# The opening of a two-layer diffusion backbone: x loaded first, modulation blocks into free buffers, the norm in two halves among three projections

## The chip, the cores and the metric

The kernel runs on one core of a Trainium2 chip. The metric is the device time of one execution in microseconds, as the median of some runs; lower is better. The engines are TensorE (PE, with its weight loads as PEld), VectorE (DVE), ScalarE (ACT), GpSimd (POOL) and SyncE (SP, which here issues most of the DMAs). SBUF holds the tiles, PSUM takes the products of PE.

## The reference, cut to what matters

Two layers over 512 latent tokens and, in the first layer, 256 context tokens, 1024 channels wide. The opening of a layer is a modulated RMSNorm and one wide input projection:

```python
sc = jax.nn.silu(c)
scc = jax.nn.silu(c_ctx)
sh1, sc1, g1, sh2, sc2, g2 = [m[:, None, :] for m in jnp.split(sc @ ada_w[l] + ada_b[l], 6, axis=-1)]
csh1, csc1, cg1, csh2, csc2, cg2 = jnp.split(scc @ ada_w[l] + ada_b[l], 6, axis=-1)
hl = rms_norm(xl, norm1_g[l]) * (1.0 + sc1) + sh1
hc = rms_norm(xc, norm1_g[l]) * (1.0 + csc1) + csh1
pl = jnp.split(hl @ w_in, IN_OFFSETS, axis=-1)   # and hc @ w_in
```

Three token mixers (window attention, a bidirectional mLSTM, a Hyena long convolution whose filters are computed from a small sine network) use the projections; their outputs are gated, merged and projected, and a convolutional feed-forward follows. The second layer has no context at its end.

## The kernel before, in words

Activations lie with channels on the partitions: x is 8 tiles (k = 0 to 7) of 128 channels by 768 tokens, columns 0 to 511 latent, 512 to 767 context. Each projection (`proj`, `gemm_part`) takes one tile of 128 output channels: a weight of 128 x 1024 is loaded (`raw`, L392), split into a rounded part wh on ACT (L342) and a rest wl on DVE (L343), and multiplied with the like parts hh and hlo of the normed x. That makes three matmuls for each k (`kstep`, L406), 24 for the 512 latent columns and 24 shorter ones for the 256 context columns.

The modulation vectors are products of silu(c) with the blocks of ada_w. A block has 512 outputs; blocks 0 and 1 are the shift, 2 and 3 the scale of the first norm, for k = 0 to 3 and 4 to 7. `ada` (L478) computes one block: four loads of 512 KB through the four buffers "wr", eight matmuls in four column groups of the array, a copy (L482), four transposes (L486) and a sum on DVE (L489); `ada_end` makes A = (1 + scale) * g (L500). The other blocks of the layer come later, row by row on DVE (`ada_rows`, L514), and read silu(c) from `silb`, which holds it along the free axis on all partitions.

The opening of the first layer (`main`) loads x on GpSimd's queue (L1677), runs blocks 0, 2, 1, 3, with the sums of squares behind block 0, the norm of k = 0 to 3 behind block 2 and of k = 4 to 7 behind block 3, and then `proj_first`: three projections, two of them k by k together and the third behind them, then the context columns of all three. Squares of the latent columns run on ACT, of the context columns on GpSimd (`SQP`).

Beside this, lanes of other work are spent in program order. A lane is a generator that yields its cost; `tick` counts the PE time of what was just issued and lets each lane run on by that time multiplied by its rate. The lane `filters` (rate 1.587 in the first layer) builds the Hyena filters: two sine stages (L594 to L606), then for each of four units of two lengths the taps (`filter_taps`: L693 and L694 on PE, times a decay on DVE L681, absolute values on ACT L685, their sum on GpSimd L689, a matmul with ones L700, a reciprocal L703) and the transform (`filter_dft`, L749), whose sums go to DRAM as gd (L766). The lane `ml_gates` (L1258 to L1350) makes the mLSTM's gates. In the opening, where no projection runs, the table START says what each yield of `ada` counts as. From program order a scheduler makes the order of each engine's queue; each engine runs its queue in order.

The first layer's gate phase ends with the pool "mixa0" (tags T and H); the attention projections write their first tile, k (L773), in the pool that takes its place, once every tile of the old pool is done with. The PSUM pool "psg" has three banks for projections.

Of the kernel before, what the change touches and what calls it, by code (L numbers as in the profile page):

```python
# [11 lines left out]
F32 = mybir.dt.float32  # L12
F32R = mybir.dt.float32r
BF16 = mybir.dt.bfloat16
AF = mybir.ActivationFunctionType
# [226 lines left out]
class Prog:  # L242
# [5 lines left out]
    START = (0.8, 0.5, 0.2, 0.8)  # L248
# [106 lines left out]
    clock = 0.0  # L355

# [38 lines left out]
    def weight(self, src, n=1024):  # L395
        raw = self.raw(src, n)
# [27 lines left out]
    def proj_first(self, l, ms, parts):  # L424

        ws = [self.weight(self.a["wA"][l, m]) for m in ms]
# [4 lines left out]
        for i, (lo, hi, _) in enumerate(parts):  # L431
# [3 lines left out]
            for group in ((0, 1), (2,)) if i == 0 else ((0,), (1,), (2,)):  # L435
                for k in range(KD):
                    for j in group:
                        self.kstep(pss[j], ws[j], slice(k * P, k * P + P), self.hlh[k], self.hll[k], lo, hi, k == 0, k == KD - 1)
                    self.tick(3 * len(group) * max(0.109, (hi - lo) * 0.422e-3))
            for o, ps in zip(outs, pss):  # L440
                o.append((lo, hi, ps))
# [28 lines left out]
    def ada(self, l, blocks):  # L470

        nc = self.nc
        for b in blocks:
            ps = self.M("adap")
            for q in range(2):
                aw = [self.raw(self.a["adaw"][b, 2 * q + j]) for j in range(2)]
                for g in range(4):
                    nc.tensor.matmul(ps[32 * g:32 * g + 32, :], self.sil[:, 4 * q + g, :],  # L478
                                     aw[g // 2][:, (g % 2) * 512:(g % 2) * 512 + 512], start=(q == 0), stop=(q == 1))
                yield 6.0  # L480
            ev = self.H("adae")
            nc.scalar.copy(ev, ps)  # L482
            yield 1.5
            p2 = self.M("adaq")
            for c in range(4):
                nc.tensor.transpose(p2[:, c * P:(c + 1) * P], ev[:, c * P:(c + 1) * P], self.ident)  # L486
            yield 1.0
            m = self.mod[l][:, b * 4:b * 4 + 4, :]
            nc.vector.tensor_reduce(m, p2.rearrange("p (c g r) -> p c r g", g=4, r=32)[:, :, 0:2, :], axis=AX.X, op=ALU.add)  # L489
            self.ada_end(l, b, 2)  # L490
# [1165 lines left out]
    def main(self, out):  # L1656
# [3 lines left out]
        for l in range(DEPTH):  # L1660
# [7 lines left out]
            with tc.tile_pool(name=f"mixa{l}", bufs=1) as self.mp, self.psum(5) as self.pm:  # L1668
                self.nT, self.nH = self.SIZES[f"A{l}"]
                if l == 0:  # L1670
# [5 lines left out]
                    for k in range(KD):  # L1676
                        nc.gpsimd.dma_start(x[k], xd[:, k, :])  # L1677
# [137 lines left out]
```

## Time and profile before

| | us |
|---|---|
| three runs: median (lowest to highest) | 2728.38 (2725.72 to 2732.3) |
| profiled execution, its own time | 2726.24 |
| its span, first to last instruction | 2724.2 |
| PE busy | 2570.0 (94%) |
| DVE busy | 1890.5 (69%) |
| ACT busy | 1039.2 (38%) |
| GpSimd busy | 298.9 (11%) |

A share is an average over the whole span. The page also cuts the span into 40 slices of 68 us; PE's digits are 5 in the first slice and 8 in the second, and 9 in most of the others. A window of the trace gives the same for any stretch, with the clock that PE was granted in it as a share of 2.4 GHz. In a timeline row the bracket at the end says how long the engine had been idle before, and what released it.

### The profile page before, as it was taken

Reading aid. Unit: us, or ns where it says so; the run is one execution under the profiler, and the core shown is the slowest. Engines: PE = TensorE matmul, PEld = TensorE weight load, DVE = VectorE, ACT = ScalarE, POOL = GpSimd, SP = SyncE. Lnnn points to the kernel's source line nnn. Section 1 sums busy time; section 2 is a strip of 40 time slices with the busy share of each in tenths; the row PEclk is TensorE's granted clock in tenths of the full one; section 3 lists DMA queues with packets and bytes.
Section 4 is the critical chain, followed back from the end, with each engine's and each line's share of the span. In section 5 each row is a group of like instructions: output and inputs, shape, how many; then the busy total and the mean of one; then the engine's idle time right before and its main releaser. Section 6 shows DMA issues by size and latency. Waiting matters only on the chain. (4 is left out here: it accounts for less than half of the span.)

```text
span 2724.2 us, 37645 instructions
## 1 busy us (share of the span) xinstructions
PE 2570.0 (94%) x14338; PEld 2171.1 (80%) x14338; DVE 1890.5 (69%) x3317; ACT 1039.2 (38%) x1874; POOL 298.9 (11%) x305
## 2 busy tenths in 40 slices
PE   5898999999999998999999998999998989999998
PEld 2677788888787787888888887877887878888887
DVE  6796676677567856978877657766376577666656
ACT  4333344455322224433333235444354233533333
POOL 3352120000000301101101001310000002000000
PEclk8899999999999998999999999999999999999999
DMA  7344452232547531343434225543335565233332
GB/s 266 111 144 138 157 138 63 63 107 96 192 149 244 187 111 39 115 127 93 125 107 124 78 62 189 184 130 101 93 121 181 178 213 185 78 93 100 94 100 62
DMA packets 153795, 349.97 MB, mean 128 GB/s; under 512 B 15681, under 2 KB 53038, under 8 KB 153488
## 3 DMA queue, kind: packets, MB, share of 16 engines
q1 hardware_dynamic: 132976, 319.03, 36.2%
q0 software_dynamic: 20640, 28.54, 4.2%
q8 instruction: 113, 1.85, 0.3%
q14 instruction: 66, 0.54, 0.1%
HBM read 288.59 MB, written 52.17 MB: 125 GB/s over the span
## 5 line engine op out<-in xcount | busy, mean ns | idle before, releaser
L406 PE MATMUL pg<-hh,wh 128*128 128x512 f32 (+1 forms) x2536 | 916.6, 362 | 21.1 <-ACT hh L342 11.0
L406 PE MATMUL pg<-hlo,wh 128*128 128x512 f32 (+1 forms) x2536 | 903.0, 356 | 2.9 <-DVE hlo L343 2.8
L406 PE MATMUL pg<-hh,wl 128*128 128x512 f32 (+1 forms) x2536 | 901.0, 356 | 0.3 <-DVE wl L343 0.3
L406 PEld LDWEIGHTS pg<-hh,wh 128*128 128x128 f32 x2536 | 484.4, 191 | 87.2 <-ACT hh L342 12.5
L342 ACT CAST wh<-wr 128x1024 fp32r<-128x1024 f32 x294 | 308.8, 1050 | 615.0 <-PE pg L406 580.4
L406 PEld LDWEIGHTS pg<-hlo,wh 128*128 128x128 f32 x2536 | 485.8, 192 | 65.0 <-DVE hlo L343 5.2
L406 PEld LDWEIGHTS pg<-hh,wl 128*128 128x128 f32 x2536 | 484.4, 191 | 64.8 <-issue 1.6
L343 DVE TENSOR_TENSOR wl<-wr,wh 128x1024 fp32r<-128x1024 f32 x294 | 366.1, 1246 | 190.5 <-ACT wh L342 185.6
L1570 DVE SCALAR_TENSOR_TENSOR x<-pg,mod,x 128x512 f32<-128x512 f32 (+1 forms) x242 | 148.2, 628 | 102.2 <-PE pg L406 96.1
L406 PE MATMUL pg<-fh,wh 128*128 128x512 f32 (+1 forms) x544 | 193.4, 356 | 11.7 <-DVE x L1570 10.3
L406 PE MATMUL pg<-fl,wh 128*128 128x512 f32 (+1 forms) x544 | 191.7, 353 | 0.0
L406 PE MATMUL pg<-fh,wl 128*128 128x512 f32 (+1 forms) x544 | 190.5, 351 | 0.9 <-DVE wl L343 0.9
L781 ACT ACTIVATE u<-pg,sv 128x512 f32<-128x512 f32 (+1 forms) x165 | 116.1, 706 | 102.3 <-PE pg L406 102.0
L782 DVE SCALAR_TENSOR_TENSOR u<-pg,sv,u 128x511 f32<-128x511 f32 (+1 forms) x165 | 108.1, 657 | 64.4 <-ACT u L781 64.3
L406 PEld LDWEIGHTS pg<-fh,wh 128*128 128x128 f32 x544 | 103.7, 191 | 30.7 <-DVE x L1570 13.7
L514 DVE SCALAR_TENSOR_TENSOR wr<-wr,silb 128x1024 f32<-128x1024 f32 x80 | 98.3, 1229 | 36.8 <-DMA wr<-in_adat 36.4
L406 PEld LDWEIGHTS pg<-fh,wl 128*128 128x128 f32 x544 | 103.7, 191 | 15.1 <-DVE wl L343 1.4
L406 PEld LDWEIGHTS pg<-fl,wh 128*128 128x128 f32 x544 | 104.0, 191 | 13.9 <-issue 0.5
L406 PE MATMUL pg<-bh,wh 128*128 128x512 f32 (+1 forms) x320 | 111.1, 381 | 3.7 <-DVE y L1556 2.0
L783 DVE SCALAR_TENSOR_TENSOR u<-pg,sv,u 128x511 f32<-128x511 f32 (+1 forms) x165 | 108.5, 660 | 2.1
L1111 ACT ACTIVATE p<-s,sm 128x512 f32<-128x512 f32 (+2 forms) x80 | 55.2, 689 | 128.9 <-DVE sm L1108 100.2
L406 PE MATMUL pg<-bh,wl 128*128 128x512 f32 (+1 forms) x256 | 94.4, 369 | 0.0
(315 smaller groups left out, 4085.1 us busy)
## 6 DMA issues: line engine op xcount, KB each, us to landing
wr<-in_wA SPq DMA_DIRECT2D x222, 512.0 KB, 3.6
wr<-in_adat SPq DMA_DIRECT2D x80, 512.0 KB, 3.6
wr<-in_wD SPq DMA_DIRECT2D x48, 512.0 KB, 3.7
wr<-in_wB SPq DMA_DIRECT2D x24, 512.0 KB, 4.7
gates<-gt SPq DMA_DIRECT2D x28, 384.0 KB, 2.3
gc<-in_g POOLq DMA_DIRECT2D x40, 256.0 KB, 3.5
g<-gd SPq DMA_DIRECT2D x40, 256.0 KB, 4.4
g<-gates SPq DMA_DIRECT2D x24, 384.0 KB, 5.9
```

The costliest lines, as they stand in the source:

```text
L342: nc.scalar.copy(h, src)
L343: (nc.gpsimd if pool else nc.vector).tensor_tensor(l, src, h.bitcast(F32), op=ALU.subtract)
L406: self.nc.tensor.matmul(ps[:, :hi - lo], a[:, ks], b[:, lo:hi], start=(first and i == 0), stop=(last and i == 2))
L514: nc.vector.scalar_tensor_tensor(prod, aw, 1.0, self.silb[:, v, :], op0=ALU.mult, op1=ALU.mult, accum_out=self.mod[l][:, b * 4 + c, v:v + 1])
L781: nc.scalar.activation(dst[:, lo:hi], ps[:, :n], AF.Identity, bias=b, scale=w(1))
L782: V(dst[:, lo + 1:hi], ps[:, 0:n - 1], w(0), dst[:, lo + 1:hi], op0=mul, op1=add)
L783: V(dst[:, lo:hi - 1], ps[:, 1:n], w(2), dst[:, lo:hi - 1], op0=mul, op1=add)
L1111: nc.scalar.activation(t[:, :w], src, AF.Exp, bias=sm[:, 2 + j:3 + j], scale=0.125, accum_out=sm[:, 4 + j:5 + j])
L1570: self.nc.vector.scalar_tensor_tensor(x[m][:, lo:hi], ps[:, :hi - lo], self.mod[l][:, p * 8 + m, j:j + 1], x[m][:, lo:hi], op0=ALU.mult, o ...
```

## The change

The opening of the first layer becomes a function `start`, and `ada` is cut in three (`ada_load`, `ada_products`, `ada_take`). x is loaded on SP's queue, ahead of all blocks. All four blocks are loaded at once into buffers that are free then: block 0 into "wr", block 2 into "wh" and "wl", block 1 into eight "HL" tiles, block 3 into eight "T" tiles; the first three weights are issued ahead of block 3. The products of block 0 come before the sums of squares, the norm of the latent columns of k = 0 to 3 follows blocks 0 and 2. `proj_first` takes the three projections together, k outermost, and calls hooks behind k = 0 (the products of block 3), k = 1 (its modulation, the latent norm of k = 4 to 7 and the norm of all context columns) and k = 7 (constants and the lane of the other blocks). `silb` is no longer computed: the finished silu(c) is written to DRAM and read back to all partitions. START has one entry, used once.

```diff
-    START = (0.8, 0.5, 0.2, 0.8)
+    START = (0.8,)
...
-    def weight(self, src, n=1024):
-        raw = self.raw(src, n)
+    def weight(self, src, n=1024, raw=None):
+        raw = self.raw(src, n) if raw is None else raw
...
-    def proj_first(self, l, ms, parts):
-
-        ws = [self.weight(self.a["wA"][l, m]) for m in ms]
+    def proj_first(self, l, ms, parts, hooks=None):
+
+
+        raws = self.early or [None] * 3
+        self.early = None
+        ws = [self.weight(self.a["wA"][l, m], raw=r) for m, r in zip(ms, raws)]
...
-            for group in ((0, 1), (2,)) if i == 0 else ((0,), (1,), (2,)):
+            for group in ((0,), (1,), (2,)) if i else ((0, 1, 2),) if hooks else ((0, 1), (2,)):
                 for k in range(KD):
                     for j in group:
                         self.kstep(pss[j], ws[j], slice(k * P, k * P + P), self.hlh[k], self.hll[k], lo, hi, k == 0, k == KD - 1)
                     self.tick(3 * len(group) * max(0.109, (hi - lo) * 0.422e-3))
+                    if i == 0 and hooks and k in hooks:
+                        hooks[k]()
...
+    def ada_load(self, b, tiles):
+
+        parts, k = [], 0
+        for t in tiles:
+            n = t.shape[1] // 512
+            o = (k % 2) * 512
+            self.nc.sync.dma_start(t, self.a["adaw"][b, k // 2, :, o:o + n * 512])
+            parts += [t[:, i * 512:i * 512 + 512] for i in range(n)]
+            k += n
+        return parts
+
+    def ada_products(self, aw):
+
+        ps = self.M("adap")
+        for k in range(KD):
+            g = k % 4
+            self.nc.tensor.matmul(ps[32 * g:32 * g + 32, :], self.sil[:, k, :], aw[k], start=(k < 4), stop=(k >= 4))
+        return ps
+
+    def ada_take(self, l, b, ps):
+        nc = self.nc
+        ev = self.H("adae")
+        nc.scalar.copy(ev, ps)
+        p2 = self.M("adaq")
+        for c in range(4):
+            nc.tensor.transpose(p2[:, c * P:(c + 1) * P], ev[:, c * P:(c + 1) * P], self.ident)
+        m = self.mod[l][:, b * 4:b * 4 + 4, :]
+        nc.vector.tensor_reduce(m, p2.rearrange("p (c g r) -> p c r g", g=4, r=32)[:, :, 0:2, :], axis=AX.X, op=ALU.add)
...
     def silu_rows(self):
-        nc = self.nc
-        nc.gpsimd.dma_start(self.silb.rearrange("p v k -> p (v k)"), self.a["cb"].rearrange("v k -> (v k)").partition_broadcast(P))
+
+        nc = self.nc
+        d = self.dp.tile([2, D], F32, name="sild")
         for v in range(2):
-            s = self.silb[:, v, :]
-            t = self.wp.tile([P, 1024], F32, tag="wr", name=self.uid("wr"), bufs=self.WB[0])
-            nc.scalar.activation(t, s, AF.Tanh, scale=0.5)
-            nc.vector.scalar_tensor_tensor(s, t, 1.0, s, op0=ALU.add, op1=ALU.mult)
-            nc.vector.tensor_scalar(s, s, 0.5, None, op0=ALU.mult)
+            nc.gpsimd.dma_start(d[v].rearrange("(k p) -> p k", p=P), self.sil[:, :, v])
+        nc.gpsimd.dma_start(self.silb.rearrange("p v k -> p (v k)"), d.rearrange("v k -> (v k)").partition_broadcast(P))
...
+    def start(self, xd):
+
+        nc = self.nc
+        lat, cx = self.parts(0)
+        x = [self.T("x") for _ in range(KD)]
+        for k in range(KD):
+            nc.sync.dma_start(x[k], xd[:, k, :])
+        wt = lambda tag, n: [self.wp.tile([P, 1024], F32, tag=tag, name=self.uid(tag), bufs=self.WB[tag != "wr"]) for _ in range(n)]
+        aw = {}
+        aw[0] = self.ada_load(0, wt("wr", 4))
+        aw[2] = self.ada_load(2, wt("wh", 3) + wt("wl", 1))
+        aw[1] = self.ada_load(1, [self.hp.tile([P, NT], F32, tag="HL", name=self.uid("aw"), bufs=16)[:, :512] for _ in range(KD)])
+        self.early = [self.raw(self.a["wA"][0, m]) for m in (M_MO, M_MO + 1, M_MO + 2)]
+        aw[3] = self.ada_load(3, [self.T("aw")[:, :512] for _ in range(KD)])
+        self.tick(self.START[0])
+        p0 = self.ada_products(aw[0])
+        self.silu_rows()
+        sums = [self.square_sums(x, lo, hi, self.SQP[j]) for lo, hi, j in self.parts(0)]
+        rs = self.rstd_of(sums)
+        p2 = self.ada_products(aw[2])
+        self.ada_take(0, 0, p0)
+        low, high = range(0, 4), range(4, 8)
+        ts = {k: self.norm_scale(x, lat, rs[0], k) for k in low}
+        self.ada_take(0, 2, p2)
+        self.hlh, self.hll = [None] * KD, [None] * KD
+        for k in low:
+            self.hlh[k], self.hll[k] = self.HL("hh"), self.HL("hlo")
+        self.norm_part(0, 1, x, lat, rs[0], low, ts)
+        p1 = self.ada_products(aw[1])
+        self.ada_take(0, 1, p1)
+        state = {}
+
+        def products():
+            state["p"] = self.ada_products(aw[3])
+
+        def rest():
+            th = {k: self.norm_scale(x, lat, rs[0], k) for k in high}
+            self.ada_take(0, 3, state["p"])
+            for k in high:
+                self.hlh[k], self.hll[k] = self.HL("hh"), self.HL("hlo")
+            self.norm_part(0, 1, x, lat, rs[0], high, th)
+            self.norm_part(0, 1, x, cx, rs[1])
+
+        def then():
+            self.load_consts()
+            self.spawn(1 / 15, self.ada_rows(0, range(4, 12)), stays=True)
+
+        return {0: products, 1: rest, 7: then}
...
-                    x = [self.T("x") for _ in range(KD)]
-                    for k in range(KD):
-                        nc.gpsimd.dma_start(x[k], xd[:, k, :])
-                    self.norm_alloc()
-                    for i, b in enumerate((0, 2, 1, 3)):
-                        for _ in self.ada(0, (b,)):
-                            self.tick(self.START[i])
-                        if i == 0:
-                            rs = self.rstd_of([self.square_sums(x, lo, hi, self.SQP[j]) for lo, hi, j in self.parts(0)])
-                        if i % 2:
-                            for r, part in zip(rs, self.parts(0)):
-                                self.norm_part(0, 1, x, part, r, range(2 * i - 2, 2 * i + 2))
-                    self.load_consts()
-                    self.silu_rows()
-                    self.spawn(1 / 15, self.ada_rows(0, range(4, 12)), stays=True)
+                    hooks = self.start(xd)
```

GpSimd (POOL) at its opening, before; sv, fg, maskb are constants, sq the squares of the context columns:

```order
L301 DMA sv_86<-in_sv 128x305 [waits DMASW0_49]
L302 DMA fg<-in_fg 128x8 [waits DMASW1_49]
L303 DMA maskb<-in_masks 128x256 [waits DMASW2_49]
L523 DMA silb<-in_cb 128x2048 [waits DMASW3_49]
L540 TENSOR_TENSOR sq_219<-x_122 128x256
L540 TENSOR_TENSOR sq_221<-x_123 128x256
```

and now:

```order
L540 DMA sild<-sil 128x8x1 [waits DVE_49] x2
L302 DMA fg<-in_fg 128x8
L303 DMA maskb<-in_masks 128x256
L541 DMA silb<-sild 128x2048 [waits DMASW2_49,DMASW1_49]
L552 TENSOR_TENSOR sq_237<-x_122 128x256 [waits DMAHW5_49]
L552 TENSOR_TENSOR sq_239<-x_123 128x256 [waits DMAHW6_49]
```

The load of x is gone from this queue, and the squares stand behind the read of silb, which waits for the two writes sild.

PE around the first three projections, before; adap is a block's product, adaq its transposes, pm with w3h and w3l the filter's taps, pg the projections:

```order
L478 MATMUL adap_359<-wr_384,sil 32x512
L693 MATMUL pm_390<-w3h_378,hd_348 128x512 [waits DVE_49,PE_49,Activation_49]
L694 MATMUL pm_390<-w3l_379,hd_348 128x512 [waits DVE_49]
L693 MATMUL pm_399<-w3h_378,hd_348 128x512 [waits PE_49]
L694 MATMUL pm_399<-w3l_379,hd_348 128x512
L486 MATMUL adaq_402<-ident,adae_393 128x128 [waits Activation_49]
L486 MATMUL adaq_402<-ident,adae_393 128x128 x3
L693 MATMUL pm_412<-w3h_378,hd_348 128x512 [waits PE_49]
L694 MATMUL pm_412<-w3l_379,hd_348 128x512
L406 MATMUL pg_488<-hh_138,wh_472 128x512 [waits Activation_49]
L406 MATMUL pg_488<-hlo_146,wh_472 128x512
```

and now:

```order
L407 MATMUL pg_354<-hh_304,wh_342 128x512 [waits Activation_49]
L407 MATMUL pg_354<-hlo_305,wh_342 128x512 [waits DVE_49]
L407 MATMUL pg_355<-hh_304,wh_346 128x512 [waits Activation_49]
L407 MATMUL pg_355<-hlo_305,wh_346 128x512
L407 MATMUL pg_354<-hh_304,wl_343 128x512 [waits DVE_49]
L407 MATMUL pg_354<-hh_306,wh_342 128x512
L407 MATMUL pg_354<-hlo_307,wh_342 128x512
L492 MATMUL adap_371<-aw_176,sil 32x512 [waits DMAHW0_49,PE_49]
L407 MATMUL pg_355<-hh_304,wl_347 128x512 [waits DVE_49]
L407 MATMUL pg_356<-hh_304,wh_350 128x512 [waits Activation_49]
L407 MATMUL pg_356<-hlo_305,wh_350 128x512
L407 MATMUL pg_356<-hh_304,wl_351 128x512 [waits DVE_49]
```

The taps have moved behind the latent projections, and the products of block 3 (adap_371) stand among the matmuls of k = 0 and 1.

PE at the end of the filter lane (pp with sdh and sdl is its last transform; pg_2731 and pg_2761 are k's projection in before, pg_2830 the context part of v's projection now), before:

```order
L749 MATMUL pp_2548<-sdl_2523,gc_2077 128x256 [waits DVE_49]
L749 MATMUL pp_2548<-sdh_2522,gc_2079 128x256
L749 MATMUL pp_2548<-sdh_2522,gc_2095 128x256
L749 MATMUL pp_2548<-sdl_2523,gc_2095 128x256
L749 MATMUL pp_2548<-sdh_2522,gc_2097 128x256
L406 MATMUL pg_2731<-hh_144,wh_2727 128x512
L406 MATMUL pg_2731<-hlo_152,wh_2727 128x512
L406 MATMUL pg_2731<-hh_144,wl_2728 128x512
L406 MATMUL pg_2731<-hh_145,wh_2727 128x512
L406 MATMUL pg_2731<-hlo_153,wh_2727 128x512
L406 MATMUL pg_2731<-hh_145,wl_2728 128x512
```

and now:

```order
L765 MATMUL pp_2607<-sdh_2577,gc_2125 128x256
L765 MATMUL pp_2625<-sdh_2596,gc_2146 128x256 [waits Activation_49]
L765 MATMUL pp_2625<-sdl_2597,gc_2146 128x256 [waits DVE_49]
L765 MATMUL pp_2625<-sdh_2596,gc_2148 128x256
L765 MATMUL pp_2625<-sdh_2596,gc_2164 128x256
L765 MATMUL pp_2625<-sdl_2597,gc_2164 128x256
L765 MATMUL pp_2625<-sdh_2596,gc_2166 128x256
L407 MATMUL pg_2830<-hh_304,wh_2801 128x256 [waits Activation_49]
L407 MATMUL pg_2830<-hlo_305,wh_2801 128x256
L407 MATMUL pg_2830<-hh_304,wl_2802 128x256
```

The last transform has moved from the middle of k's projection to behind the latent part of v's, and the next projection waits for ACT.

## Rows read from the trace of the kernel before

**Rows 1.** Windows: busy us of PE, PEld, DVE, ACT, POOL, granted clock, DMA share, GB/s.

```profile
0.00:59.20 59.20, 32.75 (x98) 9.67 (x99) 33.76 (x70) 27.96 (x44) 17.26 (x30) 0.87 0.75 273
59.20:82.60 23.40, 20.59 (x78) 15.73 (x76) 19.39 (x26) 10.13 (x19) 10.91 (x8) 0.90 0.25 83
82.60:98.30 15.70, 6.87 (x29) 6.26 (x29) 10.02 (x17) 4.72 (x9) 6.48 (x7) 0.67 0.35 85
...
120.00:200.00 80.00, 74.85 (x441) 63.85 (x440) 76.66 (x112) 30.37 (x46) 37.78 (x26) 1.00 0.41 138
200.00:240.00 40.00, 29.13 (x145) 23.26 (x145) 28.35 (x62) 18.17 (x31) 7.36 (x3) 0.87 0.35 117
240.00:320.00 80.00, 76.09 (x428) 63.75 (x426) 58.35 (x77) 25.62 (x43) 15.62 (x15) 1.00 0.47 148
320.00:345.10 25.10, 25.02 (x150) 22.38 (x151) 11.05 (x17) 5.82 (x11) 2.44 (x3) 1.00 0.52 173
```

**Rows 2.** Windows of the opening, and DMA queues (packets, MB, share of 16 engines).

```profile
10.00:20.00 10.00, 5.84 (x14) 0.67 (x16) 2.41 (x7) 0.00 (x0) 5.80 (x10) 1.00 1.04 396
...
q1 hardware_dynamic: 132976, 319.03, 36.2%
q0 software_dynamic: 20640, 28.54, 4.2%
```

**Rows 3.** Timeline of the opening: start us, us, engine, line, operation, [idle before, releaser].

```profile
3.09 19.12 SPq L392 DMA_DIRECT2D wr<-in_adaw  x8
...
34.41 1.92 PE L478 MATMUL adap<-wr,sil 128*32 128x512 f32 x16
...
36.43 0.58 ACT L482 COPY adae<-adap 128x512 f32<-128x512 f32 x1 [0.61 <-PE adap L478]
...
56.60 1.04 ACT L342 CAST wh<-wr 128x1024 fp32r<-128x1024 f32 x1 [2.03 <-DMA wr<-in_wA]
...
57.91 1.22 DVE L343 TENSOR_TENSOR wl<-wr,wh 128x1024 fp32r<-128x1024 f32 x1
...
59.62 0.63 PE L406 MATMUL pg<-hh,wh 128*128 128x512 f32 x1
```

**Rows 4.** Timeline, two projection matmuls one behind the other.

```profile
62.28 0.39 PE L406 MATMUL pg<-hh,wl 128*128 128x512 f32 x1
...
62.51 0.39 PE L406 MATMUL pg<-hh,wh 128*128 128x512 f32 x1
```

**Rows 5.** Timeline, the filter lane: a sine's first step, first tap, sums, first DFT.

```profile
33.05 0.81 DVE L594 TENSOR_SCALAR sa<-pm,sv 128x512 f32<-128x512 f32 x1
...
54.14 0.80 PE L693 MATMUL pm<-w3h,hd 128*128 128x512 f32 x1 [1.32 <-ACT w3h L342]
...
75.56 1.29 POOL L689 TENSOR_TENSOR ab<-ab,ab 128x512 f32<-128x512 f32 x1 [0.26 <-ACT ab L685]
...
91.62 0.55 PE L749 MATMUL pp<-sdh,gc 128*128 128x256 f32 x1 [8.84 <-DMA gc<-in_g]
```

**Rows 6.** Timeline, GpSimd's squares of the context columns.

```profile
12.66 3.46 POOL L540 TENSOR_TENSOR sq<-x 128x256 f32<-128x256 f32 x6
```

**Rows 7.** Timeline, mLSTM state transposes, end of the filter lane, transposes of v.

```profile
227.68 1.84 PE L1338 MATMUL pm<-mlst,ident 64*128 64x6 f32 x16
...
309.87 1.13 PE L700 MATMUL pm<-ab,ones 128*128 128x512 f32 x2 [0.40 <-POOL ab L689]
...
324.04 0.28 PE L749 MATMUL pp<-sdh,gc 128*128 128x256 f32 x1
...
328.31 0.86 ACT L773 COPY k<-pg 128x512 f32<-128x512 f32 x2 [5.19 <-DMA gd<-ghi]
...
345.09 0.82 PE L863 MATMUL pm<-ident,v 128*128 128x128 f32 x6
```

More of the change, by code (lines that the diff above doesn't have):

```diff
@@ L355 @@
     clock = 0.0
+    early = None
     def tick(self, us):
@@ L468, in ada_prepare @@
             nc.vector.tensor_scalar(self.sil[:, :, j], t[:, j * 8:j * 8 + 8], 0.5, None, op0=ALU.mult)
-    def ada(self, l, blocks):
-        nc = self.nc
[L473 to L490, printed above, removed]
+    def ada_load(self, b, tiles):
[14 more added lines that the diff above has]
+    def ada_take(self, l, b, ps):
+        nc = self.nc
+        ev = self.H("adae")
[5 more added lines that the diff above has]
+        nc.vector.tensor_reduce(m, p2.rearrange("p (c g r) -> p c r g", g=4, r=32)[:, :, 0:2, :], axis=AX.X, op=ALU.add)
+        self.ada_end(l, b, 2)
     def ada_end(self, l, b, n):
@@ L568, in norm_alloc, with norm_scale, norm_part @@
         self.hlh, self.hll = [self.HL("hh") for _ in range(KD)], [self.HL("hlo") for _ in range(KD)]
-    def norm_part(self, l, i, x, part, r=None, ks=range(KD)):
+    def norm_scale(self, x, part, r, k):
+        lo, hi, _ = part
+        t = self.H("nx")[:, :hi - lo]
+        (self.nc.gpsimd if k % 2 else self.nc.vector).tensor_tensor(t, x[k][:, lo:hi], r[:, :hi - lo], op=ALU.mult)
+        return t
+    def norm_part(self, l, i, x, part, r=None, ks=range(KD), ts=None):
         nc = self.nc
@@ L577, in norm_part @@
         for k in ks:
-            t = self.H("nx")
-            t = t[:, :n]
-            (nc.gpsimd if k % 2 else nc.vector).tensor_tensor(t, x[k][:, lo:hi], r[:, :n], op=ALU.mult)
+            t = ts[k] if ts else self.norm_scale(x, part, r, k)
             a, b = A[:, k, j:j + 1], sh[:, k, j:j + 1]
@@ L1674, in main @@
                     self.tick(0.1)
[L1675 to L1689 removed]
+                    hooks = self.start(xd)
                 else:
+                    hooks = None
                     xc = [Two(None, self.H("xc")) for _ in range(KD)]
@@ L1695, in main @@
                     self.spawn(1 / 11, self.ada_rows(l, range(4, 12)), stays=True)
-                first = self.proj_first(l, (M_MO, M_MO + 1, M_MO + 2), self.parts(l))
+                first = self.proj_first(l, (M_MO, M_MO + 1, M_MO + 2), self.parts(l), hooks)
                 self.gate_proj(l, gates, range(0, 3), first)
```

## The prediction

> **What bounds the kernel now.** I read the table of engines first: TensorE (PE) is busy 94% of the span, so outside the opening an edit gains only what it takes off PE's own queue. The row of 40 slices then shows the one place where PE is not full, its first slice. The windows over that place [rows 1] say how much: of the first 59.2 us PE idles 26.5 us, it idles 8.8 of the 15.7 us before 98.3 us, and between 200 and 240 us it idles 10.9 of 40. The clock column matters as well: 0.87, 0.90, 0.67 and again 0.87 in these windows, against 1.00 elsewhere, so part of the busy time runs at the lower of the two levels (1.2 GHz). The same rows show VectorE (DVE) busy 76.66 of 80 us between 120 and 200 us: in the first layer's gate phase DVE is the second bound, and whoever brings PE there earlier meets it.
>
> The timeline of the opening tells why PE starts late. The first projection matmul stands at 59.62 us [rows 3]. Before it come four modulation blocks, two at a time through four buffers, whose loads (2.1 MB a block) wait for the products that free the buffers; then the normed x, then the three weights.
>
> **1. The first projection matmul, from 59.6 to 37 us.** After the change SyncE issues x, then block 0, block 2, block 1, the three weights and block 3, with no buffer to wait for except that the weights follow block 0's products. SP's first big load was issued at 3.09 us [rows 3]; x now stands there. Transfers ran at 396 GB/s once both queues were full [rows 2]. x is 3.1 MB and three blocks are 6.3 MB: 9.4 / 0.396 = 24 us, so block 1 is read at 27 us. I add 2 us to landing and 3 us for the small writes discussed below: 32 us. Block 2 comes 7 us earlier, which leaves the first half of the norm its 8 us. Behind block 1 stand its last pair of products (1 us), the copy (0.58), the table load and sine of the filter (about 2) and the first weight's cast (1.04) [rows 3]: 36.6, say 37 us. The weights themselves (1.6 MB, 4 us of transfer) land just ahead of their casts. What is late next is the second weight half on DVE (1.22 us each, three of them [rows 3]).
>
> **2. From there to the mLSTM transposes, which stand at 227.68 us [rows 7].** PE's order has the same count of matmul columns before that point in both programs (299,600 and 300,200, counted from the rows of the order), so I compare what lies between. Before: 168.1 us for 275,000 columns, which at 0.226 us for 512 [rows 4] is 121.5 us; 46.6 us are lost, of them 28 us idle by the windows [rows 1], the rest low clock, the few matmuls on plain fp32 and short ones. After: from 37 us there remain 284,000 columns, 125 us, since block 3 and the filter's second stage now come after the first projection matmul. Losses after, one by one:
> - Block 3's eight products stand singly among the matmuls. Eight together took 1.92 us [rows 3]; singly they cost between that and eight times 0.96. I take 5, of which 1.8 is in the columns: +3.2.
> - Low clock after the pause before them, as the first matmul of before had it (0.63 us long, 0.39 later [rows 3, 4]): +2.5. Bounds 0 and 5.
> - The second half of the norm. Block 3's modulation now waits on DVE behind the sine chain of the filter's second stage: eight operations of 0.4 to 0.8 us [rows 5], 5 us after that stage's product, which itself stands behind the woven matmuls. I put PE's wait at +4 (bounds 0 and 8).
> - The filter's first taps. Four pairs of tap matmuls now stand together behind the latent projections; the sum over four tiles on GpSimd (three adds, 1.3 to 1.5 us) must end before the ones-matmul, which PE has in front of the context half: +6.5 and low clock again, +2. In before the like wait is the 8.84 us before 91.6 us [rows 5]; it goes.
> - Behind this, DVE's stretch as before: 5 us idle to 200 us, 9 us after it and about 4 us of low clock [rows 1], with the remaining small matmuls 7 us: +25.
>
> That is 125 + 43 = 168, so the transposes come at 205: 22.7 us earlier. DVE allows it: it starts its dense stretch about as much earlier, and 9 us of its work (two units of filter output, a modulation product) have moved behind this point.
>
> **3. From there to the transposes of v at 345.09 us [rows 7], where both orders have counted 520,320 columns.** Here part is given back. The spending of filter steps is paced by counted PE time. Before, 16 ticks of the four blocks (four each of 0.8, 0.5, 0.2 and 0.8 us in the table START, 9.2 us) drove the filter lane before the first projection; after it is one tick of 0.8 us. So the lane ends 8.4 us of PE work later: its last matmul stands at column 473,700 in before and 495,400 after. Behind the lane stands the end of the buffer pool: the copy of k, the first tile of the next pool, waits for the last filter output to be written. Before, that copy waited 5.19 us for this write and came at 328.31 us, 4 us after the last filter matmul at 324 us [rows 7], and it cost PE nothing: 55 matmuls (9.6 us) stood between, and PE was busy 25.02 of 25.10 us [rows 1]. After, nothing stands between: the next matmul in PE's order needs the bank that this copy frees. The wait is 4.6 us, from that last matmul's end at 324.3 to the end of the first copy, near 328.9. In front of it the last filter matmuls wait for their chain: from the ones-matmul at 309.87 to the last at 324.2 us it took 14 us with other DVE work between its steps; I take 10 to 14 again. PE now has 5.6 us of other work in that time (18 projection matmuls and the transform itself), so it waits 4 to 8. I take 10 us for both; the low clock behind it costs as much as the low clock of 228 to 240 us in before, up to 1 us less. So 22.7 - 10 + 1.3 = 14 us remain at 345 us. Behind it both orders are alike, and so is the rest of the time.
>
> **The sum.** The profiled execution took 2726.24 us (span 2724.2, 2.0 around it), close to the median of 2728.38. 2726.2 - 14 = 2712 us. Own range of this case: 2704 to 2721.
>
> **The one cost without a row.** The vector silu(c) is now written to DRAM and read back as rows: 2 x 1,024 elements of 4 bytes on GpSimd's queue. GpSimd then waits for them before it issues the read, and the eight squares of the context columns (3.46 us for six [rows 6]) stand behind that wait; PE's order has the sums over these squares ahead of block 2's products. So the wait has no price as long as the writes land by about 20 us. The average packet of that queue took 4.2% x 16 x 2724 / 20,640 = 89 ns [rows 2], bytes included. At nothing per element they land near 8 us. At 89 ns, and each taking turns with a packet of the bulk loads (119 ns by the like division of the other queue's 36.2% over 132,976), 128 on each engine take 27 us from 6 us on: 33 us. I take about 20: no wait, 3 us of engine time.
>
> The Trainium skill says in DMA: Bandwidth & Descriptors, Specifications, that transfers under 512 bytes are done as read-modify-write, which speaks against this write; by that rule alone the price lies toward the upper end, as in the second rival. The same page, Queues, rings and completion order, says that an engine drains a whole packet of several descriptors from one ring before it turns to the next; by that the small writes would be through after a few turns, as in the forecast. No row here shows a write of 4 bytes.
>
> **Rivals.**
> - The head start is kept. If the filter lane's end is not late enough to be waited for (DVE runs the last units faster than I allow), the 10 us are not lost: about 2701 us. For it: DVE idles 27% of 240 to 320 us [rows 1]. Against: the copy of k waits for a write whatever DVE does. Chance 0.2.
> - The small writes hold GpSimd to 33 us. Squares to 38, sums, block 2's products, its modulation at 44, the first projection at 52: 15 us of the head start go. 2727 us, no change. For it the 89 ns; against it that a few turns may do. Chance 0.18.
> - Slower: the filter lane runs by its own chain, not by PE. Its second stage's product stands behind block 3 now, so its first taps start at 67 us (37, 72 matmuls of 0.226, the first three losses above, and 4 for the gates' tanh and the cast of the filter weight) instead of 54.14 [rows 5], 13 us later. If its units then take as long as before, it ends at 337 us; the copy of k at 342, the transposes of v after 11 us of matmuls more: 353 instead of 345.1, so 2735 us. It decides once the lane loses more than 5 us against before. Against it: its units were stretched by a full DVE and PE, and get DVE earlier now. Chance 0.12.
>
> **How the numbers follow.** The forecast has 0.5. About 0.2% (5.5 us) is what a measurement of this kernel can tell from no change, so faster means under 2723 and slower over 2734. Faster: nearly all of the forecast's 0.5, the first rival's 0.2 and a little of the second, 0.70. Same: the second rival's most and edges of the others, 0.18. Slower: the third, 0.12. The range takes in the first rival's value with some room and the second's: 2697 to 2731.
>
> **What would show it.** Right: first projection matmul near 37 us; squares on GpSimd ended before 25 us; a PE wait of 4 to 6 us at the second half's first matmul and of 5 before the ones-matmul; the transposes of the mLSTM state near 205 us; a wait of about 5 us for the copy of k just behind the last filter matmul; the transposes of v near 331 us, and nothing new behind them. Wrong: squares that start after 25 us (second rival), no wait at the copy of k (first), first taps late and k copied after 340 us (third).

## The result, and the profile after

The changed kernel is slower: 2753.18 us median (2748.2 to 2758.79, four runs) against 2728.81, a ratio of 1.0090 (95% interval 1.0066 to 1.0113), some 24 us. The forecast was 2712 us, with a chance of 0.12 for slower. The profiled execution took 2752.36 us, its span is 2750.3, 26.1 more than before. Some sixteen of these are there at the transposes of v (360.7 us against 345.09 [rows 7]), the other ten come behind them, where nothing was expected.

Windows of the changed kernel, columns as in [rows 1]; the first two are, within 0.4 us, the stretches up to the first projection matmul and from there to the first tap of the filter:

```profile
0.00:48.40 48.40, 17.85 (x70) 5.04 (x70) 25.04 (x46) 17.44 (x27) 18.94 (x28) 0.97 0.96 300
48.40:80.70 32.30, 27.32 (x94) 15.21 (x94) 18.27 (x39) 16.21 (x30) 0.00 (x0) 0.94 0.33 111
120.00:200.00 80.00, 68.93 (x401) 58.85 (x400) 72.64 (x115) 30.76 (x49) 34.24 (x27) 0.96 0.43 136
200.00:240.00 40.00, 30.91 (x149) 25.73 (x150) 23.95 (x43) 11.43 (x21) 7.68 (x5) 0.79 0.31 114
240.00:320.00 80.00, 77.66 (x430) 65.86 (x429) 56.69 (x81) 31.89 (x49) 14.16 (x14) 0.98 0.49 161
320.00:360.70 40.70, 30.94 (x153) 26.22 (x152) 20.76 (x27) 8.29 (x14) 5.78 (x5) 0.79 0.30 101
```

The loss has moved. [Rows 1] had PE's idle time in front and between 200 and 240 us, and PE full from 320 us to the transposes of v; now PE idles 9.8 of the last 40.7 us before them, at a clock of 0.79, and 11.1 of the 80 us from 120, where DVE is no longer full either (72.64 against 76.66).

The opening, windows and GpSimd's timeline of the changed kernel:

```profile
10.00:20.00 10.00, 0.00 (x0) 0.00 (x0) 3.85 (x7) 1.26 (x2) 0.41 (x1) 1.00 0.98 118
20.00:30.00 10.00, 3.33 (x8) 0.41 (x8) 6.38 (x8) 3.17 (x4) 4.73 (x9) 1.00 1.02 414
```

```profile
4.52 1.82 POOL L540 DMA_DIRECT2D sild<-sil  x2 [2.12 <-DVE sil L474]
...
19.59 0.53 POOL L541 DMA_DIRECT2D silb<-sild  x1 [12.14 <-DMA sild<-sil]
20.14 4.61 POOL L552 TENSOR_TENSOR sq<-x 128x256 f32<-128x256 f32 x8
```

From 10 to 20 us, with the 4-byte writes out until 19.59, the DMA engines were 98% busy and moved 118 GB/s; once the writes had landed, 414. In the same 10 us of before it was 396 [rows 2]. So not GpSimd alone waited (12.14 us) but x too: the squares of its latent columns on ACT, each released by the load of a tile, ended 6.6 us later than in E1, which has no such writes. The last of the eight in the changed kernel, and in E1:

```profile
23.53 0.63 ACT L554 ACTIVATE sq<-x 128x512 f32<-128x512 f32 x1 [0.31 <-DMA x<-in_xT]
```

```profile
16.95 0.63 ACT L556 ACTIVATE sq<-x 128x512 f32<-128x512 f32 x1 [0.35 <-DMA x<-in_xT]
```

Milestones of the changed kernel on PE, DVE and ACT, which answer to [rows 3, 5, 7]:

```profile
48.80 0.79 PE L407 MATMUL pg<-hh,wh 128*128 128x512 f32 x1 [1.76 <-ACT wh L342]
...
60.66 0.81 DVE L610 TENSOR_SCALAR sa<-pm,sv 128x512 f32<-128x512 f32 x1 [8.38 <-PE pm L640]
...
80.71 0.49 PE L709 MATMUL pm<-w3h,hd 128*128 128x512 f32 x1 [1.99 <-ACT w3h L342]
...
88.01 2.07 PE L716 MATMUL pm<-ab,ones 128*128 128x512 f32 x2 [4.67 <-POOL ab L705]
...
226.16 2.06 PE L1354 MATMUL pm<-mlst,ident 64*128 64x6 f32 x16
...
338.01 0.58 PE L765 MATMUL pp<-sdh,gc 128*128 128x256 f32 x1 [4.63 <-ACT sdh L342]
...
341.80 0.41 PE L765 MATMUL pp<-sdh,gc 128*128 128x256 f32 x1
...
346.14 0.86 ACT L789 COPY k<-pg 128x512 f32<-128x512 f32 x2 [5.29 <-DMA gd<-ghi]
...
346.78 0.58 PE L407 MATMUL pg<-hh,wh 128*128 128x256 f32 x1 [4.56 <-ACT k L789]
```

The first projection matmul gained 10.8 us (48.80 for 59.62). The filter lane lost 26.6 at its first tap (80.71 for 54.14) and 17.8 at its last transform (341.80 for 324.04). At the end PE stands twice: 4.63 us for the lane's last step (sdh, the rounded operand of its last transform), 4.56 for the copy of k, which waits for the lane's last write.

### The profile page after: what moved, and what is told of

The parts are those of the page before. It is cut to its first block, busy times and chain, and to the rows that moved or that the text cites. A ratio compares the mean times of both kernels' runs of the same rounds, so it can differ in the third digit from the quotient of the medians.

```text
span 2750.3 us, 37660 instructions
## 1 busy us (share of the span) xinstructions
PE 2576.9 (94%) x14338; PEld 2178.1 (79%) x14338; DVE 1886.5 (69%) x3313; ACT 1040.4 (38%) x1873; POOL 285.1 (10%) x299
## 5 line engine op out<-in xcount | busy, mean ns | idle before, releaser
L407 PE MATMUL pg<-hh,wh 128*128 128x512 f32 (+1 forms) x2536 | 920.2, 364 | 21.6 <-ACT hh L342 11.4
```

Source lines behind the costliest of these rows:

```text
L407: self.nc.tensor.matmul(ps[:, :hi - lo], a[:, ks], b[:, lo:hi], start=(first and i == 0), stop=(last and i == 2))
```

## The experiments

Three possible causes of the loss were tested, alone and together. A: the 4-byte writes. B: the late filter lane, its first tap or its place in PE's order. C: the order behind the transposes of v. All milestones are starts in one profiled execution of each kernel, in us; "behind" is the time from the transposes of v to the last matmul on zt, the first step of the second layer's filter network. The ratios are against runs of the kernel before on the same chip, with a 95% interval. A profiled execution can lie off the median of its kernel: E11's is 11.1 us under it, E13's 6.9 and E6's 5.2 over it, the others within 3.5 us. So a difference of a few us between two milestones says little by itself.

| kernel | ratio (95%) | first projection | first tap | last transform | v | behind |
|---|---|---|---|---|---|---|
| before | 1 | 59.6 | 54.1 | 324.0 | 345.1 | 735.1 |
| changed | 1.0090 (1.0066 to 1.0113) | 48.8 | 80.7 | 341.8 | 360.7 | 745.3 |
| E1 | 1.0052 (1.0038 to 1.0065) | 39.8 | 72.0 | 333.5 | 352.2 | 748.6 |
| E2 | 1.0006 (0.9997 to 1.0015) | 47.2 | 57.7 | 317.6 | 338.6 | 750.3 |
| E3 | 0.9969 (0.9957 to 0.9981) | 40.1 | 51.0 | 312.5 | 333.6 | 742.2 |
| E4 | 1.0020 (1.0010 to 1.0031) | 56.8 | 76.9 | 334.7 | 353.0 | 735.6 |
| E5 | 0.9964 (0.9952 to 0.9976) | 39.4 | 49.5 | 317.0 | 338.0 | 737.6 |
| E6 | 1.0050 (1.0037 to 1.0063) | 50.3 | 83.1 | 346.1 | 364.0 | 738.7 |
| E7 | 1.0049 (1.0037 to 1.0061) | 41.7 | 75.3 | 336.7 | 355.6 | 742.2 |
| E8 | 0.9980 (0.9971 to 0.9988) | 40.3 | 51.1 | 320.7 | 341.8 | 737.4 |
| E9 | 1.0073 (1.0060 to 1.0086) | 40.1 | 72.7 | 335.7 | 356.8 | 749.0 |
| E10 | 1.0024 (1.0013 to 1.0034) | 41.5 | 51.3 | 324.6 | 343.1 | 746.2 |
| E11 | 0.9991 (0.9981 to 1.0001) | 40.4 | 51.1 | 310.8 | 331.8 | 740.5 |
| E12 | 0.9948 (0.9936 to 0.9961) | 41.0 | 44.8 | 316.7 | 337.7 | 736.5 |
| E13 | 0.9968 (0.9956 to 0.9980) | 42.2 | 44.9 | 317.6 | 344.1 | 737.0 |

**E1, rows computed (A).** `silu_rows` as before, called behind `load_consts`.

```diff
-            nc.gpsimd.dma_start(d[v].rearrange("(k p) -> p k", p=P), self.sil[:, :, v])
...
+            s = self.silb[:, v, :]
...
+            nc.scalar.activation(t, s, AF.Tanh, scale=0.5)
+            nc.vector.scalar_tensor_tensor(s, t, 1.0, s, op0=ALU.add, op1=ALU.mult)
...
```

> The changed kernel without the 4-byte writes: the rows of silu(c) are computed as before (the input read to all partitions, tanh and two VectorE operations), issued where the constants are loaded. Theory A (the small writes starved the loads, and what the opening loses the program loses): the loads of x run near 390 GB/s instead of 118, first projection matmul at 37 to 40 us instead of 48.8, and the time falls by about the same, 2753 to 2742. Theory B (the late filter lane sets the end of the gate phase): the opening comes as early as under A, but the first tap moves only with the latent projections, 80.7 to 70 us, the lane is emitted as late as now, and TensorE still stands at the copy of k: transposes of v 360.7 to 352 to 358, time 2744 to 2751.

The window from 10 to 20 us moved 410 GB/s, the first projection matmul came at 39.8 us: the writes had held the loads. But the wait at the copy of k stayed (4.6 us), as B expected, and of 9.0 us at the first projection 8.5 were left at the transposes of v and about 7 in the time (2746.32; 10 by the ratios). PE's waits of E1 from 300 to 365 us (total, times, longest):

```profile
PE pp L767 <- ACT sdh L342: 4.6, 1, 4.6
PE pg L407 <- ACT k L791: 4.6, 1, 4.6
```

**E2, pacing of before (B).**

```diff
-    START = (0.8,)
+    START = (3.2, 2.0, 0.8, 3.2)
...
         self.ada_take(0, 2, p2)
+        self.tick(self.START[1])
...
         self.ada_take(0, 1, p1)
+        self.tick(self.START[2])
+        self.tick(self.START[3])
```

> The changed kernel with the pacing of before: four ticks of together 9.2 us (3.2, 2.0, 0.8, 3.2) in the opening instead of one of 0.8 us, small writes kept. In the order the first tap then stands at PE column 34,816 instead of 57,856 and the last filter transform at 472,368 as before, instead of 493,872. Theory B: last transform near 320 us instead of 342, no wait at the copy of k, transposes of v at 335 to 345 us instead of 360.7, time 2718 to 2730. Theory A: the lane matters little, opening still starved, time 2748 to 2753.

As B expected up to the transposes of v (338.6, 22.1 earlier), with neither wait left. The time, 2733.43, missed the range by 3 us: the stretch behind took 750.3.

**E3, E1 and E2 together.** Both diffs above, nothing else.

> Both edits: rows of silu(c) computed as before and the pacing of before. If A and B each hold a part: first projection matmul at 38 to 40 us, transposes of v at 325 to 335 us, time 2705 to 2716, faster than the kernel before. If the head start of the first projection is worth nothing by itself (the lane or VectorE takes it back): transposes of v at 340 to 345 us and 2722 to 2730.

2723.8 us, faster than before, but 8 above the range and inside that of the other reading: v came as expected, and not at that reading's 340 to 345, but the stretch behind it is 7 us longer than before. E1 and E3 differ in pacing alone. From the first projection to v, in E1 and in E3:

```profile
39.80:352.10 312.30, 269.25 (x1414) 220.72 (x1415) 226.77 (x349) 115.89 (x184) 73.55 (x62) 0.92 0.41 132
```

```profile
40.10:333.60 293.50, 262.48 (x1417) 220.60 (x1418) 229.57 (x345) 111.50 (x181) 81.09 (x68) 0.92 0.43 141
```

With the lane late PE idles 43.0 us there, with the pacing of before 31.0, and nearly the same matmuls take 6.8 us longer.

**E4, the lane alone late, in the kernel before.**

```diff
-    START = (0.8, 0.5, 0.2, 0.8)
+    START = (0.05, 0.05, 0.05, 0.05)
```

> The kernel before with the table START at 0.05 four times (0.8 us in sum instead of 9.2), nothing else: the lane alone is late. In the order the last filter transform stands at PE column 493,872, as in the changed kernel. Theory B: first tap behind the latent projections (about 85 us instead of 54), a wait at the copy of k, transposes of v at 355 to 365 us instead of 345.1, time 2740 to 2755. Theory A: within 5 us of 2728.

2736.91 us: slower, with the same two waits (4.7 us for sdh, 4.5 for k) and v 7.9 later. v and the time are 2 to 3 us below B's ranges; the first projection here came 2.8 earlier. Behind v it lost only 0.5, so the ten us there belong to something else in the change. E4 and E1, both with the late lane, are 17.0 us apart at the first projection and 0.8 at v: a late lane takes a head start back.

**E5 and E6, lane of the other blocks ahead of the projections (C).** E5 is E3 with this edit (its call of `silu_rows` moves along, between the two lines), E6 the changed kernel with it alone (and the changed `silu_rows`).

```diff
-        def then():
-            self.load_consts()
-            self.spawn(1 / 15, self.ada_rows(0, range(4, 12)), stays=True)
-
-        return {0: products, 1: rest, 7: then}
+        self.load_consts()
+        self.spawn(1 / 15, self.ada_rows(0, range(4, 12)), stays=True)
+        return {0: products, 1: rest}
```

> As the run with both edits (rows of silu(c) computed as before, pacing of before), and a third: constants, rows and the lane of the other modulation blocks are issued ahead of the three projections, as in the kernel before, not behind k = 7. Theory C: the later start of this lane shifts the scheduler's order of all that follows; the four kernels with the new opening have 1,088 of the 12,508 PE instructions behind the transposes of v in other places than the kernel before (the 1,276th to the 3,539th), and take 742 to 750 us from there to the last matmul of zt in the feed-forward of the first layer (735.1 before); this kernel has none in another place. C expects 735 to 736 us for this stretch and 2712 to 2718 us in all. Rival: the stretch is long because a faster start leaves the clock lower there, or by chance of one profile; then 742 or more and 2722 to 2726.

> The changed kernel with the third edit alone: constants and the lane of the other modulation blocks issued ahead of the three projections; 4-byte writes and the single tick kept. Theory C: transposes of v stay near 360 us, the stretch from there to the last zt matmul falls from 745 to 735 or 736 us, time 2740 to 2746. Rival: all of the loss sits ahead of the transposes of v, and the time stays within 3 us of 2753.

The stretch behind v is 737.6 and 738.7 us. Its windows, in the kernel before, the changed one, and E5:

```profile
345.10:1080.20 735.10, 702.44 (x4358) 604.59 (x4357) 506.74 (x1063) 285.75 (x641) 62.55 (x71) 0.98 0.40 127
```

```profile
360.70:1106.00 745.30, 705.88 (x4358) 606.32 (x4357) 508.43 (x1068) 286.56 (x641) 60.26 (x71) 0.98 0.39 126
```

```profile
338.00:1075.60 737.60, 705.42 (x4358) 607.73 (x4357) 506.01 (x1063) 286.12 (x641) 61.67 (x71) 0.98 0.39 127
```

DVE has five instructions fewer than in the changed kernel: they stand ahead of v again, and PE's order behind v is that of before. PE idled 39 us in the changed stretch, 33 before and 32 in E5. Seven kernels with the order of before (before, E4, E5, E6, E8, E12, E13) took 735.1 to 738.7, the eight others 740.5 to 750.3. So C holds for the stretch. In the changed kernel the instructions that stand elsewhere run from 561.1 to 976.1 us, and most of the loss lies there, in the kernel before and in the changed one:

```profile
544.10:950.40 406.30, 381.94 (x2408) 334.75 (x2408) 291.10 (x644) 148.59 (x323) 38.70 (x41) 0.99 0.48 161
```

```profile
561.10:976.10 415.00, 385.02 (x2408) 336.38 (x2407) 292.79 (x647) 149.31 (x323) 36.70 (x41) 0.98 0.47 156
```

What it is worth in the time is less sure. In the profiles v came 4.4 us later in E5 than in E3 and 3.3 later in E6 than in the changed kernel, but E5's profile lies 3.2 us over its median and E3's 3.4 under. By the ratios E5 is no faster than E3, and it misses its range by 4 us; E6 gains some 11 us on the changed kernel and ends at 2745.49, inside C's range.

**E7 and E8, 16 rows of 512 bytes (A).** E7 is the changed kernel with this edit, E8 has the edits of E2 and E6 too.

```diff
-        for v in range(2):
-            nc.gpsimd.dma_start(d[v].rearrange("(k p) -> p k", p=P), self.sil[:, :, v])
...
+        ps = self.M("silp")
+        nc.tensor.transpose(ps[:16, :P], self.silt, self.ident)
...
+        nc.vector.tensor_scalar(w, ps[:16, :P], 0.5, None, op0=ALU.mult)
+        nc.gpsimd.dma_start(d, w)
```

> The changed kernel with the row of silu(c) turned by one small transpose on TensorE and scaled, and written as 16 rows of 512 bytes instead of 2,048 elements of 4 bytes; written and read back on the same queue at the same place, nothing else changed. Theory A (the number of elements starves the loads): the 10 to 20 us window moves over 380 GB/s instead of 118, first projection matmul at 38 to 42 us instead of 48.8, time 2741 to 2747, as where the rows were computed. Rival (the write and the read behind it hold GpSimd, whatever their size): window still under 200 GB/s or squares as late as now, matmul at 46 or later, 2750 to 2755.

> All three repairs with the change's own idea kept: 16 rows of 512 bytes, pacing of before (9.2 us), lane of the other blocks ahead of the projections. If A, B and C are the whole loss: first projection matmul at 38 to 41 us, transposes of v at 329 to 335 us, 735 us behind them to the last zt matmul, time 2708 to 2716, the fastest of all. If the rows' VectorE and ScalarE work, which this saves against the run with three edits, is worth nothing: equal to that run.

E7 is at 2744.25 us, with the window from 10 to 20 us at 411 GB/s. GpSimd's timeline of E7:

```profile
10.88 4.92 POOL L555 TENSOR_TENSOR sq<-x 128x256 f32<-128x256 f32 x5 [0.77 <-DMA x<-in_xT]
21.74 0.56 POOL L543 DMA_DIRECT2D sild<-silw  x1 [5.94 <-DVE silw L542]
26.82 0.55 POOL L544 DMA_DIRECT2D silb<-sild  x1 [4.53 <-DMA sild<-silw]
```

The same vector through the same queue took 5 us in rows and 15 in elements. The scheduler also put the write behind the squares, so the wait (4.53) no longer stands ahead of them, and from 10 to 20 us no such write was out at all: neither the time nor that window tells the elements from the place. The window in which the rows were out does:

```profile
21.74:26.82 5.08, 4.47 (x26) 1.62 (x26) 1.65 (x4) 2.60 (x6) 0.56 (x1) 1.00 1.04 396
```

With 16 rows of 512 bytes out, the bulk loads kept their rate. E8 (2726.03) missed its range by 10 us, at v (341.8) by 7, and is slower than E5, which spends more on ScalarE and VectorE; so is E11 than E3. Why is open.

**E9 and E10, first taps and end of the lane taken apart (B).** E9 is E1 with the first rate below, E10 is E3 with the second; the rest of the line stays as it is.

```diff
-    RATE = ({'filt': 1.587,
+    RATE = ({'filt': 1.75,
...
-    RATE = ({'filt': 1.587,
+    RATE = ({'filt': 1.45,
```

> The ticks moved two things at once, the first taps and the end of the filter lane. Here they are taken apart. Base: the changed kernel with the rows of silu(c) computed as before (2746 us), single tick kept, and the lane's rate 1.75 instead of 1.587: the first tap stays behind the latent projections (PE column 57,856), the last transform stands at 472,368 as before. Theory B1 (the lane's end decides, by the wait for the pool): PE waits less than 2 us at the copy of k, transposes of v near 335 to 340 us instead of 352, time 2724 to 2731. Theory B2 (the late first taps decide: they leave PE without work in the opening and all units late): last transform still past 328 us, transposes of v at 345 to 352 us, time 2738 to 2746.

> The other half: base is the changed kernel with the rows computed as before and the pacing of before (2724 us), with the lane's rate 1.45: the first tap stays at PE column 34,816, before the projections, the last transform stands at 493,872, as in the changed kernel. B1: transposes of v at 345 to 352 us instead of 333.6, a wait of 4 to 5 us at the copy of k, time 2735 to 2744. B2: transposes of v at 332 to 337 us, time 2722 to 2728.

E9 has its last transform at the place of before and no wait at the copy of k, and still it is slower than E1: 2749.77 us, v at 356.8, later than either theory had it. The waits are elsewhere. Window and PE's timeline of E9 (hsin is the output of a sine stage, w3h a weight of the taps; both belong to the lane):

```profile
200.00:240.00 40.00, 21.90 (x106) 17.47 (x104) 23.62 (x42) 9.01 (x15) 6.38 (x4) 0.78 0.32 113
```

```profile
234.99 1.22 PE L642 MATMUL pm<-hsin,w 64*128 64x256 f32 x2 [4.71 <-ACT hsin L624]
240.98 0.80 PE L711 MATMUL pm<-w3h,hd 128*128 128x512 f32 x1 [4.77 <-ACT w3h L342]
```

PE, in order, now waits for the lane's steps inside the gate phase. So B1 falls: the lane, started at 72.7, did not end earlier for having its steps placed earlier. E10 shows the other bound: taps at 51.3 but the end placed late, v 9.5 us later than in E3 (343.1, 2 under B1's range), both waits back (4.6 each), 2735.87 us, inside B1's range. B2 alone falls too.

**E11, E2 with the rows of 512 bytes.** The diffs of E2 and E7, with the order behind v as changed.

> The changed kernel with the pacing of before and 16 rows of 512 bytes for silu(c), constants and the lane of the other blocks behind the projections as changed. Against the run with both edits it differs in how the rows are made. If making the rows on ScalarE and VectorE (two tanh, four operations on 1,024 columns) costs the gate phase anything: transposes of v before 333 us and 2718 to 2722 us. If it costs nothing: 2722 to 2726 us as there; over 2727 the small transpose and the wait of GpSimd for its own write would cost.

v at 331.8, but 2728.1 us: by its time the transpose and the wait cost something, by its v the making of the rows did. The profiled execution (2717.02) is 11 us under the median of its kernel, so its milestones flatter it, and no row shows what costs there.

**E12 and E13, first taps still earlier.** Base E5; block 3's load stands behind the filter's loads, START as shown (E12, E13).

```diff
-        aw[3] = self.ada_load(3, [self.T("aw")[:, :512] for _ in range(KD)])
...
         self.ada_take(0, 1, p1)
+        aw[3] = self.ada_load(3, [self.T("aw")[:, :512] for _ in range(KD)])
...
-    START = (3.2, 2.0, 0.8, 3.2)
+    START = (6.2, 2.0, 0.8, 0.2)
...
+    START = (6.2, 2.0, 0.8, 3.2)
```

> Base is the run with three edits (2722 us). Block 3 is loaded behind the filter's decay and third weight instead of ahead of them, and of the 9.2 us of ticks 3 more come ahead (6.2, 2.0, 0.8, 0.2 instead of 3.2, 2.0, 0.8, 3.2): the first tap moves to PE column 15,872 from 34,816, near 41 us instead of 49.5, and the lane's last transform stays at 472,368. In thirteen kernels so far the transposes of v came 276 to 292 us after the first tap, wherever the lane's end stood in the order. If that holds (the filter lane's own chain from its first tap sets the end of the gate phase): transposes of v at 321 to 331 us instead of 338, time 2708 to 2717. If the order's end bounds it now (TensorE has the same work up to the same place): 335 to 339 and 2719 to 2725.

> As the run before it, with 3 us more of ticks in all (6.2, 2.0, 0.8, 3.2): first tap at PE column 14,336, and the lane's last transform at 460,336, 12,000 columns earlier. If the chain from the first tap sets the end: transposes of v as in the run before it, 321 to 331 us, time 2708 to 2717. If the order's end bounded that run, this one is earlier by up to the 5 us that the columns take. If VectorE, full from 55 to 80 us, sets it: both stay at 334 us or later.

v did not follow: 337.7, as in E5. This doesn't decide whether the chain from the first tap still bounds a lane that starts early, since E12's second pair of taps came at 49.7 (E5's at 50.2): its lane hardly started earlier. E13, end placed earlier, came later and not earlier, at v (344.1, in a profile 6.9 us over its median) and in time (2723.31 us), so nothing speaks for the order's end either. Both stand at 334 or later, as the reading with a full VectorE had it, but VectorE was busy 20.12 of the 25 us from 55 to 80 in E13; what holds v back there is open. E12 is nevertheless the fastest of all, 2717.98 us, 0.5% under the kernel before. Its window and that of the kernel before:

```profile
40.00:100.00 60.00, 45.74 (x219) 33.60 (x219) 47.58 (x73) 27.79 (x50) 20.96 (x20) 0.83 0.38 114
```

```profile
40.00:100.00 60.00, 41.48 (x161) 28.13 (x160) 45.10 (x70) 30.40 (x52) 18.66 (x16) 0.74 0.49 159
```

Even there PE idles 14 of 60 us: the head start at the first projection is 18.6 us at that point and 13 in the end.

## Why the prediction was wrong

The forecast was some 40 us off: 30 at the transposes of v (331 forecast, 360.7 measured), 10 behind them. By its own marks the 30 are 11.8 up to the first projection matmul (48.80 for 37), 9.4 in step 2 and 8.5 in step 3. The experiments divide them otherwise, since a late lane takes back what comes ahead of it.

- Step 3 failed, and most depends on it. It took the lane's end from its place in PE's order, "8.4 us of PE work later", and priced the lost pacing by two waits at that end, 10 us for both. The two waits were there in size (4.63 and 4.56 us). What the step put at nothing is the lane's late start: PE, in order, waits for the lane's steps all the way (43.0 us idle from the first projection to v in E1, 31.0 in E3). The lost pacing cost 18.6 us at v (E1 to E3) to 22.1 (changed to E2). The text gives no time for the last transform; from v at 331 back over the wait and 24,900 columns (11 us) I estimate 315, and it came at 341.80.
- The third rival, "the filter lane runs by its own chain", to which I gave 0.12, is what happened. From first tap to last transform the changed kernel took 261.1 us, and E1, E2, E3, E4, E6, E7, E9 and E11 257.9 to 263.0. In all but one of these nearly the same number of PE columns stands in between (436,016 or 437,552 by the places on record), so equal lengths alone show no chain. E9 does: its last step stands at column 472,368 instead of E1's 493,872, 9.5 us of matmuls less at 0.226 us for 512, and it took 263.0. That is one kernel. Where more columns stood in between it took longer, as in before (269.9), E10 (273.3), E12 and E13 (271.9 and 272.7); it was longer too in E5 and E8 (267.5 and 269.6), which have E3's places, but the lane of the other blocks ahead. The rival's start was too early (67 for 80.71) and its length too long (270 us). What within the lane takes those 260 us was not taken apart.
- The cost without a row. I took 3 us of engine time and squares without a wait. The squares ended at 24.75 us, just within the bound that I had set, yet x came late: the price fell on the bulk loads, where I hadn't looked. The first projection stood at 48.80 for 37; with the 4-byte writes alone removed it was 39.8 (E1) or 41.7 (E7). That is 5 to 8.5 us at v (E7, E1). My second rival had nearly the size (52 us) and the wrong victim: it charged GpSimd's wait.
- The Trainium skill, DMA: Bandwidth & Descriptors, Specifications, says that transfers under 512 bytes are done as read-modify-write. 118 GB/s beside 4-byte writes and 396 beside rows of 512 bytes agree with a high price below that size; that read-modify-write is the reason no row shows. By the same page of the Trainium skill, Queues, rings and completion order, I had expected the writes to be through after a few turns; they landed after 15 us, which doesn't agree with that reading.
- Step 2, from the first projection to the mLSTM transposes: 168 us forecast, 177.4 measured, and 177.9 in E1; 174.7 in E3, with the pacing of before. I had assumed DVE's dense stretch "as before" with 5 us of PE idle to 200 us; it was 11.1, with DVE not full, and, up to 362 us, PE waited 11.4 us in six places for the lane's sdh, 4.63 of them in step 3. The waits that I named were there in size: 2.6 for the second half of the norm (4 forecast), 4.67 before the ones-matmul (5), 4.56 at the copy of k (4.6).
- "Behind it both orders are alike" was wrong. The count of matmul columns is the same at that point, the order is not: 1,088 of the PE instructions behind v (12,508 by the count on record, 12,854 records in the trace) stand in other places. The lane of the other modulation blocks started 24 projection steps later and shifted all it is woven with. In the traces that costs 10.2 us; putting it back returned 4.6 and 6.6 us of the stretch (E3 to E5, changed to E6), and by the ratios about 1 and 11 us of the time.
- Two small sums don't come out: step 3 adds 1.3 us back where its text gives up to 1, and 2712 less 10 is 2702, not the first rival's 2701.

With A and B mended, v stands at 333.6 (E3), and 2723.8 us are reached. That this v is only 2.6 us from the forecast is luck: the 331 held 8.7 us for the late lane, which E3 doesn't have. Without them the forecast is 322.4, and E3 comes 11.2 later, 3 of them at the first projection (40.1 for 37). So the head start is real, but at v it is 11.5 us, half of the 22.7 that I gave it; where the other half goes was not taken apart.

## What to carry to other kernels

A chain of dependent steps that is spread through a queue in order has two ends: the place of its last step, and its start plus its own length; take the later of both, and when an edit cuts the pacing, ask first when the chain now starts. Price a DMA of few bytes by its number of elements and charge it to every transfer that is out at the same time. Equal counts of work up to a point don't make equal orders behind it: compare the orders row by row.

## What was not expected of the hardware

2,048 elements of 4 bytes on GpSimd's queue were 15 us on the way (4.52 to 19.59 us); beside them, from 10 to 20 us, 16 DMA engines were 98% busy and moved 118 GB/s, against 410 without them (E1). The same 8 KB in 16 rows of 512 bytes took 5 us (21.74 to 26.82), beside 396 GB/s. The bulk queue of these 10 us (packets, MB, share of 16 engines) in the changed kernel and in E1:

```profile
q1 hardware_dynamic: 406, 1.11, 87.1%
```

```profile
q1 hardware_dynamic: 1344, 4.10, 103.0%
```

By the division that the prediction used, a packet of the bulk queue took 343 ns beside the elements and 123 ns without them: a high busy share is no sign of a high rate.
